# Strassen's token sums before the norm's root, in place; the first two products of two pairs ahead of it; weight sums split anew in each superblock

## The chip, the cores and the metric

The kernel runs on one core of a Trainium2 chip. The core has five engines with instruction queues of their own: TensorE (PE, matrix products, with weight loads listed as PEld), VectorE (DVE), ScalarE (ACT), GpSimd (POOL) and SyncE (SP), which here issues all transfers between DRAM and the on-chip memory (SBUF). Products land in PSUM banks. The metric is the device time of one execution in microseconds (us); the kernel before took 2969.23 us, the median of 3 runs (2965.46 to 2977.01).

## What is computed

One layer of a hybrid encoder, on 2048 prompt tokens and 32 tokens of a running stream, 1024 features wide. Cut to what matters here:

```python
m, k, v, h_fin, ssm_conv_new = mixer(rmsnorm(x, p['g_mix_pre']), ...)
x = x + rmsnorm(m, p['g_mix_post'])
f, ffn_conv_new = conv_ffn(rmsnorm(x, p['g_ffn_pre']), ffn_conv_prev, p)
x = x + rmsnorm(f, p['g_ffn_post'])

def conv_ffn(h, conv_prev, p):
    gu = h @ p['w_up']
    gate, up = gu[..., :D_FF], gu[..., D_FF:]
    gate_c, conv_new = causal_dwconv(gate, conv_prev, p['ffn_conv_w'], p['ffn_conv_b'])
    act = jax.nn.gelu(gate_c, approximate=True) * up
    return act @ p['w_down'], conv_new
```

`rmsnorm(x, g)` is x times g times one over the root of the mean of x squared plus 1e-6, per token. `mixer` ends with an output projection (1024 by 1024). D_FF is 2816, in 22 units of 128. Everything is 32-bit floating point.

## The kernel before

**Precision.** PE multiplies in a rounded 32-bit format. Each operand is therefore split into a high part (a cast) and a low part (the operand less the high part); `dense` (L144 to L159) makes three products of each: high by high, high by low, low by high. A split costs an ACT cast and a subtraction on POOL or DVE (`divide`, L129, for weights; `part`, L1021, for activations).

**Stages.** `phase_in` (attention starts at about 640 us) makes queries, keys, values and the state-space half. Then tokens go in four superblocks (SBS): three of 512 tokens and one of 544. For superblock s, `Tail.stream` does the output projection in two halves of tokens (`out_units`), its norm and the residual addition (`residual`), the feed-forward norm, the up projection with its gate for 22 units j, and the down projection in groups of units (`down`). What is left of the down projection (`owed`) is done in the next superblock's stream, its first eight steps at the start and the rest after the norm. `finish` adds the second residual. The stream of superblock s is a generator: `Attention.heads` takes steps of it between the attention slots of superblock s + 1. Superblock 3 has no attention beside it (`alone`).

**Strassen.** In superblocks 1, 2 and 3 (FAST) gate and up product of a unit are made together in `pair`: the two halves of the tokens and the two halves of the features make a 2 by 2 block product with gate and up weights, done with seven products in place of eight. Products 1 and 2 use the first half's tokens alone; 5 and 3 the difference of the halves; 6, 7 and 4 sums and differences of all four quadrants (m11, m12, m21, m22). `normal` builds these: it takes the norm's root, multiplies the tiles by gain and root, splits the first half (a), and for the second half (b) subtracts, splits and files the operands in `self.X`. Products 3, 5, 6, 7 need sums of weights. Superblock 0, which uses plain products (`up`), makes them from the raw weights (`sums`) and writes them to DRAM (sS). Superblock 1 loads each, splits it and writes the split sum to DRAM (wS_sum); 2 and 3 load these (`factor`).

**Norms.** Squares are made on ACT and added tile by tile on POOL (`square`, L805) into one tile (msq, sq). `rstd_steps` (L181) multiplies it on PE with a column of ones (L192), scales on DVE (L201), takes the power -0.5 on POOL (L211) and spreads the result over the partitions with another product (L223). In superblock 0 the root is not multiplied into the tokens but into the gate after the product (L1222), and its square into the last norm (`finish`, through `cols`).

**Order.** A planner orders each engine's instructions by a simulated timeline, within the dependencies. `pin` and `mark` hold products of PE in written order: each pinned product stays behind the last marked one, so that the dense products keep their order up to superblock 2; attention's own products are marked but not pinned, and can run ahead. In superblock 3 dense products aren't pinned. Tiles with one name share a fixed number of buffers: a new one waits until all readers of the old are done. The raw weights have a ring of 5 (RBUFS), the split ones of 6 (WBUFS), xhi0 to xhi7 and xlo0 to xlo7 one each.

## Time and profile before

| | |
|---|---|
| median of 3 runs | 2969.23 us |
| profiled execution | 2973.12 us (span 2971.3 us) |
| mean granted TensorE clock | 0.967 |
| busy: PE, weight loads | 93%, 82% |
| busy: DVE, ACT, POOL | 63%, 46%, 51% |
| moved to and from DRAM | 725.20 MB, 244 GB/s |

Shares are of the span. PE's busy time is modelled from pipelined products, so that a busy PE need not be at its peak. A line of a timeline has the start and duration in us, the engine, the line of the kernel, the operation with the tile written and the tiles read, its size and its count, and in brackets the idle time ahead of it and what ended that. A line of groups has the count, busy us and mean ns of one, and the idle time ahead. A line of waits has the waiting engine and line, what was waited for, then us in all, times, and the longest. A line of transfers has count, KB each and the median us from issue to landing.

### The profile page before, as it was taken

The numbers are of one execution on the slowest core, as the hardware profiler recorded it, in microseconds if no ns is written. First come the engines' busy times: TensorE is split into PE (matmuls) and PEld (weight loads), VectorE is DVE, ScalarE is ACT, GpSimd is POOL, SyncE is SP. The second block draws the span as 40 slices with busy tenths as digits, with TensorE's granted clock in tenths as the row PEclk, the third lists the DMA queues.
The fourth block names the chain that finished last, engine by engine and source line by source line (L and its number), as shares of the span: only waits on it lengthen the run. The fifth ranks groups of instructions, "written<-read, shape, count | busy, mean of one in ns | idle before, by whom it ended". The sixth has DMA issues, their size and how long they took to land. (4 is left out here: it accounts for less than half of the span.)

```text
span 2971.3 us, 50761 instructions
## 1 busy us (share of the span) xinstructions
PE 2761.0 (93%) x18019; PEld 2451.1 (82%) x18019; DVE 1863.9 (63%) x2915; ACT 1380.9 (46%) x2920; POOL 1521.7 (51%) x1361
## 2 busy tenths in 40 slices
PE   7999999989889999988799999898999999699997
PEld 6777787877778888877689988887999999699997
DVE  7667576547686777637876764478665762634444
ACT  4344444337665555436665553465543553332222
POOL 3555565435776767648665654474422334521213
PEclk9999999989989999999899999999999999799998
DMA  5646464649778888778478898876878777698885
GB/s 177 182 153 174 146 178 126 159 134 291 242 256 285 282 283 286 277 269 270 169 263 314 312 330 294 314 234 195 294 263 276 256 245 263 219 328 267 300 277 180
DMA packets 383806, 725.20 MB, mean 244 GB/s; under 512 B 78938, under 2 KB 198370, under 8 KB 383554
## 3 DMA queue, kind: packets, MB, share of 16 engines
q1 hardware_dynamic: 383554, 721.95, 72.8%
q8 instruction: 144, 2.36, 0.3%
q14 instruction: 108, 0.88, 0.1%
HBM read 526.44 MB, written 195.36 MB: 243 GB/s over the span
## 5 line engine op out<-in xcount | busy, mean ns | idle before, releaser
L150 PE MATMUL o<-xhi,w 128*128 128x256 f32 (+2 forms) x3760 | 916.0, 328 | 37.5 <-ACT xhi L315 8.0
L150 PEld LDWEIGHTS o<-xhi,w 128*128 128x128 f32 x3760 | 648.6, 192 | 103.6 <-issue 9.1
L135 POOL TENSOR_TENSOR w<-wraw,w 128x512 fp32r<-128x512 f32 (+3 forms) x332 | 521.1, 1575 | 288.6 <-ACT w L134 258.0
L150 PE MATMUL o<-xlo,w 128*128 128x256 f32 (+2 forms) x1880 | 613.6, 326 | 6.4 <-DVE xlo L301 4.2
L700 POOL TENSOR_TENSOR beta<-beta,prow 128x512 f32<-128x512 f32 (+3 forms) x256 | 269.4, 1054 | 337.8 <-DVE prow L695 291.9
L150 PEld LDWEIGHTS o<-xlo,w 128*128 128x128 f32 x1880 | 361.2, 192 | 36.3 <-DVE xlo L301 6.1
L150 PE MATMUL o<-ah,w 128*128 128x512 f32 x992 | 343.5, 403 | 10.1 <-DMA w<-wS_dn 5.1
L134 ACT CAST w<-wraw 128x512 fp32r<-128x512 f32 (+3 forms) x332 | 226.0, 683 | 185.3 <-PE o L150 106.8
L695 DVE TENSOR_TENSOR_SCAN prow<-gam,prow,z 128x513 f32<-128x513 f32 x192 | 244.1, 1273 | 32.1 <-ACT beta L693 31.3
L868 DVE TENSOR_TENSOR wt<-pt,wt 128x512 fp32r<-128x512 f32 (+2 forms) x320 | 189.5, 598 | 105.1 <-ACT wt L867 103.7
L150 PEld LDWEIGHTS o<-ah,w 128*128 128x128 f32 x992 | 187.5, 189 | 53.6 <-DVE f L1292 5.8
L150 PE MATMUL u<-xhi,w 128*128 128x256 f32 (+1 forms) x832 | 211.9, 332 | 7.4 <-DVE y L1256 3.3
L692 ACT ACTIVATE gam<-z 128x512 f32<-128x512 f32 (+2 forms) x320 | 173.0, 541 | 77.8 <-PE z L844 45.2
L867 ACT CAST wt<-pt 128x512 fp32r<-128x512 f32 (+2 forms) x320 | 166.6, 527 | 76.9 <-PE pt L863 73.9
L885 PE MATMUL pa<-wt,v 128*64 128x256 f32 (+3 forms) x1152 | 180.6, 287 | 19.9 <-DVE wt L868 9.8
L150 PE MATMUL o<-al,w 128*128 128x512 f32 x496 | 197.4, 398 | 0.0
L863 PE MATMUL pt<-ident,beta 128*128 128x128 f32 x1088 | 182.1, 282 | 10.8 <-DVE beta L700 4.5
L885 PEld LDWEIGHTS pa<-wt,v 128*64 128x64 f32 (+1 forms) x1152 | 150.3, 168 | 38.7 <-DVE wt L868 14.0
L1184 POOL TENSOR_TENSOR y<-y,gb 128x512 f32<-128x512 f32 (+1 forms) x66 | 88.3, 1337 | 169.7 <-ACT gb L1183 169.0
L693 ACT ACTIVATE beta<-z 128x512 f32<-128x512 f32 (+2 forms) x320 | 173.3, 542 | 0.0
L844 PE MATMUL z<-k,qa 128*128 128x512 f32 (+2 forms) x320 | 141.3, 442 | 33.5 <-DVE prow L695 29.6
L150 PE MATMUL t<-ah,w 128*128 128x272 f32 (+1 forms) x768 | 165.1, 303 | 7.2 <-ACT ah L1190 4.2
(326 smaller groups left out, 5952.9 us busy)
## 6 DMA issues: line engine op xcount, KB each, us to landing
w<-wS_up SPq DMA_DIRECT2D x198, 512.0 KB, 5.4
w<-wS_sum SPq DMA_DIRECT2D x176, 512.0 KB, 5.1
w<-wS_dn SPq DMA_DIRECT2D x144, 384.0 KB, 4.2
wS_sum<-w SPq DMA_DIRECT2D x88, 512.0 KB, 6.2
w<-wS_out SPq DMA_DIRECT2D x78, 512.0 KB, 5.8
wS_up<-w SPq DMA_DIRECT2D x66, 512.0 KB, 4.1
wraw<-wup SPq DMA_DIRECT2D x88, 256.0 KB, 4.2
sS<-wraw SPq DMA_DIRECT2D x88, 256.0 KB, 3.2
```

The source lines that it names most:

```text
L134: nc.scalar.copy(hi, raw[:, :m, :])
L135: nc.gpsimd.tensor_tensor(lo, raw[:, :m, :], hi.bitcast(F32), op=ALU.subtract)
L150: mm = nc.tensor.matmul(ps[:, : c1 - c0], l, r, start=first and i == 0 and k == 0, stop=last and i == 2 and k == len(w) - 1, **({"skip_gro ...
L692: nc.scalar.activation(g[:, c0:512], z, AF.Sigmoid, scale=-0.125)
L693: nc.scalar.activation(b[:, :n], z, AF.Sigmoid, scale=0.125)
L695: nc.vector.tensor_tensor_scan(back(pr), back(g), z[:, 0:1].to_broadcast([P, n + 1]), self.kn.ones[:, 0:1] if prev is None else prev, op0= ...
L700: eng.tensor_tensor(b[:, :n], b[:, :n], pr[:, c0 + 1 : 513], op=ALU.mult)
L844: mm = nc.tensor.matmul(z[:, :n], q[:, P * b : P * b + P], k[:, :n], start=e == 0, stop=e == 1 and kc < s)
L863: mm = nc.tensor.transpose(t[:, P * j : P * j + P], w[:, P * j : P * j + P], kn.ident[:])
L867: nc.scalar.copy(hi, t)
L868: nc.vector.tensor_tensor(lo, t, hi.bitcast(F32), op=ALU.subtract)
L885: nc.tensor.matmul(av[:m, 2 * P * p + c0 : 2 * P * p + 2 * P], v[:, j, :m], wt[:, rest, j, c0:], start=kc == s and p + j + rest == 0, stop ...
```

## The change

- **Quadrants in tiles of their own.** `Q` holds four tiles n0 to n3 (half by half of features) where `M` was one; differences are made in place in them, and the operands for products 6, 7 and 4 go to tiles n0 to n6.
- **No root ahead of the sums.** In FAST superblocks `residual` leaves the residual h in the x tile, and ACT writes h times the gain back to the quadrant. `near` splits the first half, `far` subtracts and splits for the second; both split into the tiles of the output projection's input (`cat`) where `normal` and `split` took new ones. `root` sums the squares, which ACT makes in place in the eight h tiles, with eight products per block; POOL's additions go. The output projection's norm sum gets its last square as a second term.
- **Root after the product.** In `pair` the gate is multiplied with the root: its first half on DVE in place of ACT's copy, its second half by one more operation on POOL. The last norm takes the root's column as superblock 0 does.
- **Order.** In FAST superblocks the rest of `owed` comes right after `far`; then the root's sum (pinned), products 1 and 2 of pairs 0 and 1 (AHEAD), and the root's spreading (pinned). `bank` keeps their PSUM banks apart. In superblock 0 the first half's split and root go into the second half of the projection.
- **Weights.** The split sums are written no more; superblocks 1, 2 and 3 each load the raw sums and split them. RBUFS is 4. The tiles msq and sq share one name, and attention takes its own later.

```diff
 WBUFS = 6
-RBUFS = 5
+RBUFS = 4
 FAST = (1, 2, 3)
+AHEAD = 2
...
             for i, t in enumerate(sq):
-                nc.tensor.matmul(
+                mm = nc.tensor.matmul(
                     ps[:q, b : b + 1], t[:, b * P : b * P + q], self.ones[:, 0:1],
                     start=i == 0, stop=i == len(sq) - 1,
                 )
+                if pin and b + i == 0:
+                    self.pin(mm)
+        if pin:
+            self.mark(mm)
...
                 nc.vector.tensor_tensor(att[-1][r, :512], av[0:64, :], att[-1][r, :512], op=ALU.add)
+                if h == 1:
+                    sq = self.tmp.tile([P, 544], F32, name="sq")
...
         if c0 == 0:
-            self.M = self.mp.tile([P, KC, 544], F32, name="m")
-            self.m = [self.M[:, c, :] for c in range(KC)]
-            self.msq = att.tmp.tile([P, 544], F32, name="msq")
+            self.Q = [[self.mp.tile([P, 4, 272], F32, name=f"n{2 * i + e}") for e in range(2)] for i in range(2)]
+            self.msq = att.tmp.tile([P, 544], F32, name="sq")
...
+            nc.scalar.copy(m, ps[:, : c1 - c0])
+            if i < KC - 1:
+                att.square(self.msq[:, c0:c1], m, i == 0)
+            else:
+                t = att.tmp.tile([P, 272], F32, name="sqt", bufs=2)[:, : c1 - c0]
+                nc.scalar.activation(t, m, AF.Square)
+                self.msqs = [self.msq[:, c0:c1], t]
             yield
...
+    def m(self, c, half):
+        c0, c1 = half
+        return self.Q[int(c0 > 0)][c // 4][:, c % 4, : c1 - c0]
 
...
-            eng.tensor_tensor(m[:, c0:c1], m[:, c0:c1], x, op=ALU.add)
-            nc.sync.dma_start(kn.hS[s][:, c, c0:c1], m[:, c0:c1])
-            att.square(self.msq[:, c0:c1], m[:, c0:c1], c == 0, x)
+            h = x if fast else m
+            eng.tensor_tensor(h, m, x, op=ALU.add)
+            nc.sync.dma_start(kn.hS[s][:, c, c0:c1], h)
+            if fast:
+                nc.scalar.activation(m, h, AF.Copy, scale=kn.col(C_GFFN + c))
+            else:
+                nc.scalar.activation(x, m, AF.Square)
+            self.h.append(x)
             yield
...
         kn, nc, att = self.kn, self.kn.nc, self.att
         c0, c1 = half
         if c0 == 0:
-            self.x = kn.parts()
+            self.x = self.cat
...
+            yield
+
+    def root(self, s, half, pin=False):
...
-        kn.rstd_narrow(att.tmp, *kn.bank, [self.msq[:, c0:c1]], c1 - c0, D, out=self.r[:, c0:c1], rcol=col)
         self.cols[s, c0] = col
+        yield from kn.rstd_steps(
+            att.tmp, *kn.bank, self.h, c1 - c0, D, out=self.r[:, c0:c1], rcol=col, pin=pin
+        )
 
...
-    def normal(self, s, half):
-
...
+    def squares(self):
+        for h in self.h:
+            self.kn.nc.scalar.activation(h, h, AF.Square)
+
+    def near(self, s, half):
+
+        kn, nc = self.kn, self.kn.nc
+        c0, c1 = half
+        hi, lo = self.x = self.cat
+        for k in range(KC):
+            self.part(self.m(k, half), hi[k][:, c0:c1], lo[k][:, c0:c1], nc.vector if k % 2 else None)
+            yield
+
+    def far(self, s, half):
+
+        kn, nc = self.kn, self.kn.nc
         c0, c1 = half
         n = c1 - c0
...
+        (b11, b21), (b12, b22) = self.Q
+        two = slice(0, 2), slice(2, 4)
+        sub = lambda out, a, b, k: nc.vector.tensor_tensor(out[:, k, :n], a[:, k, :n], b[:, k, :n], op=ALU.subtract)
+        for k in two:
+            sub(b12, b12, b11, k)
+        for k in range(KC):
+            self.part(self.m(k, half), hi[k][:, c0:c1], lo[k][:, c0:c1], nc.vector if k >= 4 else None)
         self.X = {}
-        for i, src in zip(put, raw):
-            h, l = put[i][:, :, :n], put[i][:, :, n : 2 * n]
-            for e in range(2):
-                k = slice(2 * e, 2 * e + 2)
-                self.part(src[e], h[:, k, :], l[:, k, :], nc.vector)
-            self.X[i] = [h[:, k, :] for k in range(4)], [l[:, k, :] for k in range(4)]
+
+        def put(i, src, h, l, eng):
+            h, l = (self.mp.tile([P, 4, 272], F32R, name=f"n{e}") for e in (h, l))
+            self.part(src[:, :, :n], h[:, :, :n], l[:, :, :n], eng)
+            self.X[i] = [h[:, k, :n] for k in range(4)], [l[:, k, :n] for k in range(4)]
+
+        for k in two:
+            sub(b22, b22, b12, k)
+        put(6, b22, 2, 4, nc.vector)
+        for k in two:
+            sub(b11, b22, b11, k)
+        for k in two:
+            sub(b21, b22, b21, k)
+        put(7, b11, 3, 5, nc.gpsimd)
+        put(4, b21, 0, 6, nc.vector)
         side = lambda ks, c: ([hi[k][:, c : c + n] for k in ks], [lo[k][:, c : c + n] for k in ks])
         self.X |= {1: side(range(4), 0), 2: side(range(4, 8), 0), 3: side(range(4, 8), n), 5: side(range(4), n)}
 
...
-        key = ("sum", j, i)
-        if key in kn.kept:
-            return kn.recall(self.ring(), [key], 4, self.slot())
-        return kn.divide(self.ring(), kn.raw(self.raws[j, i][:], 4), 4, key if s < NSB - 2 else None, self.slot())
+        return kn.divide(self.ring(), kn.raw(self.raws[j, i][:], 4), 4, None, self.slot())
...
-        k = self.n_bank % (5 if self.keep else 3)
+        k = max(self.n_bank, 0) % (5 if self.keep else 3)
...
-        for i in (1, 2, 5, 6, 3, 7, 4) if j == 0 else (1, 5, 6, 2, 3, 7, 4):
+        for i in (1, 2, 5, 6, 3, 7, 4) if j < AHEAD else (1, 5, 6, 2, 3, 7, 4):
...
             elif i == 2:
-                nc.scalar.copy(gb[:, 2 : 2 + h], b)
+                nc.vector.tensor_tensor(gb[:, 2 : 2 + h], b, self.r[:, :h], op=ALU.mult)
             elif i == 3:
                 e = min(nt, 512) - h
-                add(gb[:, 2 + h : 2 + h + e], b[:, :e], t[:, :e])
+                add(t, b, t)
+                mul = lambda out, c: nc.gpsimd.tensor_tensor(out, t[:, c], self.r[:, h:nt][:, c], op=ALU.mult)
+                mul(gb[:, 2 + h : 2 + h + e], slice(0, e))
                 if last:
-                    add(gb[:, 516:548], b[:, e:], t[:, e:])
+                    mul(gb[:, 516:548], slice(e, h))
...
+    def ready(self, s, half):
+        if s in FAST:
+            self.squares()
+            yield from self.near(s, half)
+        else:
+            yield from self.split(s, half)
+        yield from self.root(s, half)
...
-        chain = chained(self.residual(s, a), self.normal(s, a) if fast else ())
+        chain = chained(self.residual(s, a), self.ready(s, a))
         for n, _ in enumerate(self.out_units(s, cat, b)):
             yield
-            if n % 4 == 0 or fast and n % 4 == 2:
+            if n % 2 == 0:
                 next(chain, None)
         for _ in chain:
...
-        if not fast:
-            self.root(s, a)
-        for _ in self.residual(s, b):
-            pass
+        self.finished(self.residual(s, b))
+        early = []
         if fast:
-            for _ in self.normal(s, b):
-                pass
+            self.squares()
+            self.far(s, b)
+            yield from owed
+            root = self.root(s, b, pin=True)
+            next(root)
+            acts = {0: []}
+            self.n_bank = -4
+            early = [self.pair(s, j, acts[0]) for j in range(AHEAD)]
+            for p in early:
+                yield from islice(p, 4)
+            next(root)
         else:
-            self.split(s, a)
-            self.split(s, b)
-            self.root(s, b)
-        yield from owed
+            self.finished(self.split(s, b))
+            self.finished(self.root(s, b))
+            yield from owed
+            acts = {0: []}
         done = iter(())
```

75 lines of the change are left out of this document (26 added, 49 removed).

## Prediction

> **What bounds the kernel now.** I read the page first: the span, and PE's busy share in forty slices.
>
> ```profile
> span 2971.3 us, 50761 instructions
> ...
> PE   7999999989889999988799999898999999699997
> ```
>
> TensorE (PE) is the bound: busy in nine tenths or more of nearly every slice. A change gains where PE is empty or at half clock, and costs where it gives PE work or stops feeding it. Slices 12, 20, 28 and 35 (74 us each) hold the places where a superblock passes from the output projection to the feed-forward network (I call them **transitions**). I then read the busy time of each engine in those stretches. The columns are stretch, length, busy us (instructions) of PE, weight loads, DVE, ACT, POOL, then granted clock, DMA share, GB/s.
>
> ```profile
> 840.00:870.00 30.00, 18.79 (x78) 14.23 (x77) 28.16 (x48) 18.34 (x47) 18.94 (x22) 0.67 0.64 217
> 1380.00:1450.00 70.00, 50.71 (x274) 38.24 (x273) 63.73 (x89) 49.54 (x114) 47.36 (x54) 0.86 0.45 152
> 1970.00:2030.00 60.00, 46.32 (x261) 36.75 (x260) 56.68 (x84) 42.29 (x99) 42.96 (x49) 0.93 0.48 152
> 2530.00:2600.00 70.00, 47.18 (x260) 43.05 (x258) 43.75 (x87) 21.09 (x54) 40.53 (x49) 0.73 0.65 207
> ```
>
> I count as lost the length less PE busy times the clock: 30 - 18.79*0.67 = 17.4 for superblock 0, 70 - 50.71*0.86 = 26.4 for 1, 60 - 46.32*0.93 = 16.9 for 2, 70 - 47.18*0.73 = 35.6 for 3: **96 us** in all. The timelines of superblock 3 (start, duration, engine, line) show what the loss is made of.
>
> ```profile
> 2521.48 0.29 PE L150 MATMUL t<-xhi,w 128*128 128x272 f32 x1
> ...
> 2545.42 0.29 PE L150 MATMUL t<-xhi,w 128*128 128x272 f32 x1
> 2556.69 1.15 PE L192 MATMUL u<-ones,msq 128*128 128x1 f32 x6 [10.98 <-POOL msq L805]
> ```
> ```profile
> 2527.18 3.28 ACT L1024 CAST xhi<-m 128x272 fp32r<-128x272 f32 x8 [4.46 <-DVE m L1038]
> ```
> ```profile
> 2547.54 0.43 DVE L992 TENSOR_TENSOR m<-m,xr 128x272 f32<-128x272 f32 x1
> ...
> 2560.71 3.36 DVE L1038 SCALAR_TENSOR_TENSOR m<-m,cv,u 128x272 f32<-128x272 f32 x8 [2.61 <-issue]
> 2563.98 1.30 DVE L1051 TENSOR_TENSOR m<-m 128x1088 f32<-128x1088 f32 x1
> ...
> 2582.03 0.71 DVE L1025 TENSOR_TENSOR t<-ub,t 128x544 fp32r<-128x544 f32 x1
> ```
> ```profile
> 2553.39 3.25 POOL L805 TENSOR_TENSOR msq<-msq,xr 128x272 f32<-128x272 f32 x4
> ...
> 2563.37 3.44 POOL L1025 TENSOR_TENSOR xlo<-m,xhi 128x272 fp32r<-128x272 f32 x3 [4.27 <-ACT xhi L1024]
> ```
>
> The output projection ends at 2521.8. Only then does ACT cast the *first* half's tiles (2527.18): `normal` takes a new generation of the xhi and xlo tiles, of which there is one each, and the projection still reads the old one. The residual's last addition ends at 2547.97. PE, busy until then with the down projection still owed, stands from 2545.7 and gets the sum of squares only at 2556.69, when POOL has added the last squares (L805). Root and broadcast last until 2560.7, then eight multiplications on DVE, a subtraction, splits and two more levels of differences, the last split (t) ending at 2582.7. Superblock 1 has the same chain between attention slots:
>
> ```profile
> 1388.29 0.41 DVE L992 TENSOR_TENSOR m<-m,gb 128x256 f32<-128x256 f32 x1
> ```
> ```profile
> 1423.65 0.50 PE L192 MATMUL u<-ones,msq 128*128 128x1 f32 x4
> ...
> 1451.23 0.28 PE L150 MATMUL o<-xhi,w 128*128 128x256 f32 x1
> ```
>
> The residual's last addition ends at 1388.7, the sum starts 35 us later, and the first product behind it runs at 1451.23. Outside the transitions PE is nearly full:
>
> ```profile
> 890.00:1290.00 400.00, 396.66 (x1901) 323.08 (x1900) 275.83 (x342) 203.41 (x426) 270.39 (x220) 1.00 0.82 283
> 1460.00:1900.00 440.00, 411.05 (x2840) 373.29 (x2839) 279.26 (x391) 226.92 (x486) 258.36 (x220) 0.99 0.87 310
> 2060.00:2440.00 380.00, 376.57 (x2664) 346.88 (x2663) 248.21 (x363) 178.93 (x386) 129.27 (x123) 1.00 0.80 269
> 2650.00:2900.00 250.00, 249.22 (x1982) 248.81 (x1981) 109.86 (x233) 61.59 (x134) 52.80 (x45) 1.00 0.83 285
> ```
>
> Idle there is 400 - 396.66 = 3.3 us in superblock 0's feed-forward part, 29.0 in 1's, 3.4 in 2's, 0.8 in 3's. Superblock 1 differs from 2 in that it splits the weight sums and writes them; that is the state into which the change puts 2 and 3, without the writes.
>
> **The change part by part.** The sum is made against the profiled execution, 2973.1 us (span 2971.3), which is 3.9 above the median of the runs shown, 2969.2.
>
> *Transitions.* Two things change. First, the splits are written into the projection's own input tiles, so the first half's casts, low parts and root no longer wait for the projection's end; they go under its second half, where PE is full and the other engines aren't. Second, the subtractions no longer wait for the root: the residual times the gain goes straight to them (L1038's multiplications go, ACT scales instead), the squares go to ACT, and PE sums eight square tiles where POOL did seven additions. In superblock 3 the second takes 2556.6 - 2548.0 = 8.7 us of POOL, 4.1 of root and broadcast and 3.4 of multiplications off the products' path, 16 us; the first takes the 3.3 us of casts, with their low parts, from in front of the residual, which can add some 5 us earlier, near 2543. Left are one subtraction (1.3) and the first splits (3.44 us for three low parts on POOL here), so product 5 can run near 2548; then three more subtractions at 1.3 and whole-tile casts and low parts of about 3 us each in turn, the last near 2560 instead of 2582. PE fills from 2545.7 with two products of two pairs: 48 matmuls, by the last stretch above (250 us for 1982) 0.126 us each, 6 us. Of 35.6 lost I take away 26, leaving some idle and about 10 us of half clock. In superblock 1 attention shares DVE (63.7 of 70 busy); the difference chain, some 10 us of DVE (four subtractions at 1.3, and low parts), takes about 20 there, so products near 1405 instead of 1451: 20 of 26.4, and in proportion, rounded down, 12 of 16.9 in superblock 2. Superblock 0 gains by the first half's splits alone: 9 of 17.4. **-67**, bounds -30 and -86 (all but 10).
>
> A wait is added here: the squares overwrite h, so ACT must wait for h's way to DRAM.
>
> ```profile
> w<-wS_sum SPq DMA_DIRECT2D x176, 512.0 KB, 5.1
> wS_sum<-w SPq DMA_DIRECT2D x88, 512.0 KB, 6.2
> ...
> hS<-m SPq DMA_DIRECT2D x48, 128.0 KB, 4.2
> ```
>
> That is 4.2 us to landing, and behind a waiting square stand ACT's casts for the differences and attention's sigmoids; for these squares waits the sum, and in superblocks 1 and 2, where PE's order is fixed, both pairs' early products behind the sum. The down projection still owed by the superblock before covers it; without that cover it costs 4 us each, inside the bounds.
>
> The TensorE clock shows in the rows: 0.73 over superblock 3's transition. The Trainium skill, page "TensorE: Matmul & The Clock Gate", section "What's actually happening", says that an idle window of about 3.4 us halves the clock; if no gap that long were left, superblock 3 would keep full clock, and by that rule the sum would be 5 us lower (half of the 10 us that I left at half clock). The trace agrees so far that a gap of 11 us stands ahead of the low clock.
>
> *More work on PE.* Each root sums eight tiles instead of one, and the output norm's sum gets a second term.
>
> ```profile
> 2520.69 0.63 PE L192 MATMUL u<-ones,msq 128*128 128x1 f32 x6
> 2521.26 0.39 PE L150 MATMUL t<-xlo,w 128*128 128x272 f32 x1
> ```
>
> Six instructions take 2521.26 - 2520.69 = 0.57, 0.095 each; two per block and tile. Added: 28 for each half of 256 tokens (six), 42 for each of 272 (two), and 4 or 6 more for the second term: 252 + 36 = 288, 27 us. The first halves' 13.7 fall between dense products and count whole; of the second halves' I count 5, since PE is empty there otherwise. **+19**, bounds 14 and 27.
>
> *Weight sums.* Gone: 88 writes and 176 loads of 512 KB, the loads now 176 of 256 KB raw. In superblock 1 PE waited for loads, and SP's queue stood behind those writes:
>
> ```profile
> PE o L150 <- DMA w<-wS_up: 6.6, 7, 2.1
> ...
> PE o L150 <- DMA w<-wS_dn: 5.1, 1, 5.1
> ```
> ```profile
> SPq L138 <- POOL w L135: 81.8, 47, 6.6
> ```
>
> 11.7 us of PE's 29.0; superblock 2, with neither splits nor writes, idles 3.4 in all. I take **-9** (0 to -12). Added in superblocks 2 and 3: 88 splits each, at the cost shown in 1:
>
> ```profile
> L135 POOL TENSOR_TENSOR w<-wraw,w 128x512 fp32r<-128x512 f32 x83 | 115.8, 1406 | 51.1 <-ACT w L134 46.5 <-DMA w<-wS_up 4.2 <-DMA wraw<-sS 0.4
> ...
> L1166 POOL TENSOR_TENSOR ub<-ub 128x256 f32<-128x256 f32 x22 | 17.5, 795 | 13.6 <-DVE ub L1133 11.3 <-DVE rn_v L201 1.3 <-DMA wS_sum<-w 1.1
> ```
> ```profile
> L134 ACT CAST w<-wraw 128x512 fp32r<-128x512 f32 x81 | 49.8, 621 | 63.4 <-PE o L150 52.4 <-DMA wS_sum<-w 5.5 <-PE u L150 4.3
> ```
>
> That is 88 * (1.406 POOL + 0.621 ACT) = 124 and 55 us in each. POOL rises in superblock 2's stretch from 129 to 129 + 76*1.406 + 19*0.795 = 251 of 380 (66%; 1 has 59%), in 3's from 53 to 149 of 250. Both fit, but POOL works in order: a split stands behind y's product (waiting for ACT's sigmoid), and attention's beta product behind splits. Of superblock 1's 29.0 idle, 17 is not loads; I carry half, **+8** (0 to 25) for 2 and, with no attention there, **+3** (0 to 45) for 3.
>
> DVE pays too. The gate's taps in superblock 1, then in 2:
>
> ```profile
> L1177 DVE SCALAR_TENSOR_TENSOR y<-gb,cv,y 128x512 f32<-128x512 f32 x44 | 49.9, 1134 | 15.1 <-ACT y L1175 14.7
> ...
> L1185 DVE TENSOR_TENSOR y<-ub,y 128x512 f32<-128x512 f32 x22 | 24.6, 1119 | 24.0 <-POOL y L1184 24.0
> ```
> ```profile
> L1177 DVE SCALAR_TENSOR_TENSOR y<-gb,cv,y 128x512 f32<-128x512 f32 x38 | 31.9, 840 | 7.0 <-ACT y L1175 6.6
> ...
> L1185 DVE TENSOR_TENSOR y<-ub,y 128x512 f32<-128x512 f32 x19 | 14.7, 774 | 7.1 <-POOL y L1184 7.1
> ```
>
> (1.134 - 0.840)*44 + (1.119 - 0.774)*22 = 20.5 us of DVE per superblock, on 248 of 380: covered by DVE's idle time.
>
> *Raw ring of four.* Superblock 0 holds four raw tiles per step until the sums are out; the fifth served for loading ahead.
>
> ```profile
> SPq L114 <- DMA sS<-wraw: 35.8, 40, 2.8
> ```
>
> SP already waits for a release 40 times, yet PE idles 3.3 us in 400. **+3**, bounds 0 and 25 (1.1 us in each of 22 steps).
>
> *Gate in the pair.* One copy moves from ACT to DVE; a POOL multiplication of 0.8 us (L1166's kind) enters the gate's chain, hidden while the pair's results are used a group later. At the very end it isn't:
>
> ```profile
> PE t L150 <- ACT ah L1190: 4.2, 1, 4.2
> ```
>
> **+1** on that wait (0 to 2). The dearer last scale with the root's column, and the shared sq tile, cost nothing: they lie beside dense work.
>
> Sum: -67 + 19 - 9 + 8 + 3 + 3 + 1 = **-42**; 2973.1 - 42 = 2931, and 2927 against the median.
>
> **The rivals.** (1) *The transitions close.* Only 10 us of the 96 stay: -86 in place of -67, -61 in all, 2908. For it: 20 us of chain gone and 6 us of early work in each. Against: DVE at 91% in superblock 1's. (2) *The gain arrives by half.* The squares wait for h's landing, the sum holds the fixed order, the early products come no earlier than their successors would: -30, and SP's waits only change their names (0 for -9): -30 + 19 + 8 + 3 + 3 + 1 = +4, 2973. (3) *POOL late with the splits, slower.* Superblock 2 takes 1's idle rate, 29.0*380/440 = 25, and in superblock 3 each of 22 pairs waits for two splits in a row, 2*(1.406 + 0.621) = 4.1 us: 89. Then -67 + 19 - 9 + 25 + 89 + 3 + 1 = +61, 3030. With 25 in superblock 2 it decides from (67 - 19 + 9 - 25 - 3 - 1)/22 = 1.3 us of wait per pair on. For it: POOL's queue is in order; against: the split's own waits (46.5 us on ACT) hurt PE little in 1. (4) *DVE shut out.* If each split stopped a DVE operation of two SBUF inputs for its whole length, superblock 2 would get 88*1.406 = 124 on DVE's 248 of 380: DVE full, and PE would lose as in a transition; taking a tenth of 380, +38 for +8, 2957. The rows speak against it: 20.5 us, not 124. This is the rule of the Trainium skill, "SBUF — State Buffer", section "Who interferes with whom": a DVE instruction with two SBUF inputs and a POOL instruction that reads SBUF block each other entirely; the trace shows the lengthening, but an overlap only now and then.
>
> **How the numbers follow.** Forecast 0.42 (its own range 2915 to 2950), rival 1 0.20, rival 2 0.17, rival 3 0.15, rival 4 0.06. About 0.5%, 15 us, is what a measurement of this kernel tells from no change, so faster means under 2954, slower over 2984. Faster: 0.39 of the forecast, rival 1 whole, 0.02 of 4: 0.61. Slower: 0.14 of rival 3 and 0.03 of rival 2: 0.17. The rest 0.22. The range from 2900 to 2990 leaves out some 0.07 at rival 1's end and 0.13 at rival 3's; the bounds of the transitions, the ring and superblock 2's splits, one at a time, lie inside it, superblock 3's 45 too.
>
> **What would show it.** Right: in superblock 3 the first half's casts run under the output projection, the last difference split ends within 20 us of the residual's last addition (35 now), the transitions lose 30 us or so, superblock 1's load waits shrink, PE idle in 2's and 3's stretches stays below 12. Wrong: PE waiting for L135 in superblocks 2 or 3, DVE above 80% there, PE gaps in superblock 0's steps behind SP's releases, or the root's sum standing in front of idle PE.

## The result, and the profile after

The changed kernel takes **2983.38 us** (median of 8 runs, 2980.06 to 2989.66) beside 2972.86 for the kernel before on the same chip (8 runs, 2965.46 to 2977.01): ratio **1.0038** [1.0026, 1.0051]. It is slower by 0.4%, less than the 0.5% that the prediction counted as no change. I forecast 2927, 1.4% faster; the measured time lies in the range (2900 to 2990), which reaches to both sides of the kernel before, but on the other side of it. Below, every run stands by its ratio to the kernel before on the same chip; 0.1% is 3 us.

First the changed kernel's page (span, and PE's busy share in forty slices).

```profile
span 2980.7 us, 51672 instructions
...
PE   7999999989899999999899999998999999789997
```

Slices 12, 20, 28 and 35, the transitions, show 9, 8, 8 and 7 (8, 7, 8 and 6 before); slice 36, just behind the last of them, fell from 9 to 8. The transitions by the columns of the prediction (stretch, length, busy us of PE, weight loads, DVE, ACT, POOL, clock, DMA share, GB/s):

```profile
840.00:870.00 30.00, 26.08 (x155) 22.68 (x154) 24.76 (x45) 19.94 (x50) 14.46 (x16) 0.83 0.77 259
1375.00:1445.00 70.00, 65.86 (x436) 58.27 (x435) 58.13 (x80) 49.90 (x123) 53.64 (x57) 0.95 0.66 214
1945.00:2005.00 60.00, 56.45 (x360) 50.86 (x359) 54.79 (x77) 42.65 (x101) 43.67 (x42) 0.91 0.52 170
2510.00:2580.00 70.00, 60.29 (x415) 55.23 (x413) 45.52 (x68) 31.14 (x73) 56.57 (x55) 0.97 0.66 207
```

Length less PE busy times the clock gives 30 - 26.08*0.83 = 8.4, 70 - 65.86*0.95 = 7.4, 60 - 56.45*0.91 = 8.6 and 70 - 60.29*0.97 = 11.5: **36 us lost in place of 96**. (Of superblock 3's 11.5, some 5 are the start of the gap of 6.36 us that is followed below and that runs past the end of this stretch.) The transitions shorten as the change meant them to. The same view of the feed-forward stretches shows who took it back.

```profile
880.00:1280.00 400.00, 384.16 (x1821) 310.95 (x1819) 255.80 (x325) 194.41 (x405) 249.84 (x209) 0.99 0.78 269
1450.00:1860.00 410.00, 397.33 (x2773) 363.65 (x2772) 290.96 (x406) 215.12 (x460) 260.79 (x232) 0.98 0.67 216
2020.00:2440.00 420.00, 409.98 (x2882) 376.42 (x2881) 310.66 (x426) 234.05 (x494) 265.20 (x235) 0.99 0.64 206
2560.00:2620.00 60.00, 42.94 (x294) 41.53 (x294) 44.35 (x60) 22.15 (x48) 48.45 (x44) 0.86 0.68 224
2620.00:2930.00 310.00, 297.55 (x2313) 294.79 (x2312) 152.73 (x256) 105.06 (x213) 176.19 (x152) 0.98 0.62 198
```

PE idles 15.8 us in superblock 0 (3.3 before), 12.7 in 1 (29.0), 10.0 in 2 (3.4) and 17.1 + 12.5 = 29.5 in 3 (before, 2.0 in the 60 us from 2595, where its pairs begin, and 0.8 in the 245 behind them, at a clock of 1.00). In superblock 3 the clock fell with the gaps, to 0.86 in the first 60 us. There POOL is busy 48.45 of 60 and 176.19 of 310 us; before it was 52.80 of 250. The worst gap of superblock 3, in the timelines of PE, then ACT, then DVE, shows how it arises:

```profile
2581.24 0.59 PE L151 MATMUL t<-xhi,w 128*128 128x272 f32 x1 [6.36 <-ACT ub L1176]
```
```profile
2580.26 0.65 ACT L1216 CAST ah<-y 128x544 fp32r<-128x544 f32 x1 [6.68 <-DVE y L1213]
2580.81 0.38 ACT L1176 COPY ub<-t 128x272 f32<-128x272 f32 x1
```
```profile
2570.00 7.92 DVE L1345 SCALAR_TENSOR_TENSOR f<-f,cv,rstd 128x256 f32<-128x256 f32 x8
2577.85 1.21 DVE L1211 TENSOR_TENSOR y<-ub,y 128x512 f32<-128x512 f32 x1
2578.98 1.25 DVE L1213 TENSOR_TENSOR y<-ub,y 128x32 f32<-128x32 f32 x1
```

PE stood 6.36 us for an ACT copy that frees a PSUM bank (`ub`, L1176). That copy stood in ACT's queue behind the cast of a gate (`ah`, L1216), that cast waited for DVE's gate product (L1211, L1213), and the product stood in DVE's queue behind eight multiplications of the finish (L1345), 7.92 us together. All three operations are longer here than elsewhere. In the kernel before, the eight multiplications take 4.71 us, and in the changed kernel's next pair, with POOL idle beside it, the second product (L1213) takes 0.19:

```profile
2585.24 4.71 DVE L1319 SCALAR_TENSOR_TENSOR f<-f,cv,rstd 128x256 f32<-128x256 f32 x8 [0.24 <-ACT rstd L229]
```
```profile
2591.81 0.19 DVE L1213 TENSOR_TENSOR y<-ub,y 128x32 f32<-128x32 f32 x1
```

In the gap that product, of 32 columns, took 1.25 us and ended at 2580.2, just when the split that POOL ran beside it ended (start 2578.47, 1.71 us). It was held, not slowed. So the question for the experiments was which part of the change makes DVE late, and what the other costs are.

### The profile page after: what moved, and what is told of

Its sections match the earlier page's. It is cut to its first block, busy times and chain, and to the rows that moved or that the text cites. A ratio compares the mean times of both kernels' runs of the same rounds, so it can differ in the third digit from the quotient of the medians.

```text
span 2980.7 us, 51672 instructions
## 1 busy us (share of the span) xinstructions
PE 2791.3 (94%) x18307; PEld 2485.9 (83%) x18307; DVE 1947.4 (65%) x2920; ACT 1464.4 (49%) x3075; POOL 1770.3 (59%) x1552
## 5 line engine op out<-in xcount | busy, mean ns | idle before, releaser
L136 POOL TENSOR_TENSOR w<-wraw,w 128x512 fp32r<-128x512 f32 (+3 forms) x508 | 768.1, 1520 | 401.3 <-ACT w L135 372.4
L135 ACT CAST w<-wraw 128x512 fp32r<-128x512 f32 (+3 forms) x508 | 335.0, 663 | 314.9 <-PE o L151 136.6
L709 POOL TENSOR_TENSOR beta<-beta,prow 128x512 f32<-128x512 f32 (+3 forms) x256 | 261.8, 1024 | 233.0 <-DVE prow L704 202.3
L877 DVE TENSOR_TENSOR wt<-pt,wt 128x512 fp32r<-128x512 f32 (+2 forms) x320 | 190.3, 598 | 83.6 <-ACT wt L876 82.9
L151 PE MATMUL o<-n,w 128*128 128x256 f32 (+1 forms) x1404 | 190.3, 285 | 4.3 <-DVE y L1157 2.5
L1203 DVE SCALAR_TENSOR_TENSOR y<-gb,cv,y 128x512 f32<-128x512 f32 (+1 forms) x132 | 169.7, 1285 | 27.3 <-ACT y L1201 20.4
L151 PEld LDWEIGHTS o<-n,w 128*128 128x128 f32 x1404 | 179.0, 190 | 6.0 <-DVE y L1157 2.8
```

The costliest lines, as they stand in the source:

```text
L135: nc.scalar.copy(hi, raw[:, :m, :])
L136: nc.gpsimd.tensor_tensor(lo, raw[:, :m, :], hi.bitcast(F32), op=ALU.subtract)
L151: mm = nc.tensor.matmul(ps[:, : c1 - c0], l, r, start=first and i == 0 and k == 0, stop=last and i == 2 and k == len(w) - 1, **({"skip_gro ...
L709: eng.tensor_tensor(b[:, :n], b[:, :n], pr[:, c0 + 1 : 513], op=ALU.mult)
L877: nc.vector.tensor_tensor(lo, t, hi.bitcast(F32), op=ALU.subtract)
L1203: nc.vector.scalar_tensor_tensor(y[:, :W], gb[:, i : i + W], kn.col(wc + i), y[:, :W], op0=ALU.mult, op1=ALU.add)
```

## The experiments

### What the split weight sums cost, and how

Four kernels: the changed one with the sums kept again; the kernel before without keeping them; and two that keep one part of each split and make the other, so that ACT's cast and POOL's subtraction are apart.

```diff
-        return kn.divide(self.ring(), kn.raw(self.raws[j, i][:], 4), 4, None, self.slot())
+        key = ("sum", j, i)                      # e1: as before the change
+        if key in kn.kept:
+            return kn.recall(self.ring(), [key], 4, self.slot())
+        return kn.divide(self.ring(), kn.raw(self.raws[j, i][:], 4), 4, key if s < NSB - 2 else None, self.slot())
```

> The changed kernel with one part undone: the split weight sums are kept again (superblock 1 splits them and writes both parts to DRAM, superblocks 2 and 3 load them back). Theory A (the transitions gave what they were to give, and the gain was spent on the splits in superblocks 2 and 3): superblock 3's stretch of pairs loses some 20 us of TensorE time again in place of 60, superblock 2's some 18 in place of 33, superblock 1's some 43 in place of 31, so the time falls by 40 to 50 us to about 2938 us (2928 to 2950). Rival B (the gate's new multiplications by the root, on POOL and DVE, slow the pairs whatever the weights do): superblock 3 still loses 50 us or more and the time stays at 2970 to 2985 us.

2951.72 us, ratio 0.995 [0.9934, 0.9966]: 0.88% below the changed kernel, **26 us**. Theory A holds in kind; the fall is less than its 40 to 50 us.

```diff
 # e3: in the kernel before
-        ... 4, key if s < NSB - 2 else None, self.slot())
+        ... 4, None, self.slot())
```

> The kernel before with one part of the change alone: no split weight sum is kept, superblocks 1 to 3 each load the raw sum and split it. Theory A (the splits by themselves cost superblock 3 some 40 us and superblock 2 some 15, and superblock 1 gains some 10 from the writes that fall away): about 3015 us (3000 to 3030). Rival B (only together with the multiplications by the root do the splits overload POOL, DVE and ACT): 2965 to 2985 us.

2980.41 us, 1.0035 [1.0017, 1.0053]: 10 us. That is inside rival B's range and far below theory A's, but the reason that B gives, that the splits cost only together with the multiplications by the root, is not what the stages show. The table has the us from the first tap of one superblock to the first tap of the next, by the profiled execution of each kernel (a **tap** is one of the two operations per pair on DVE that make the gate's convolution, L1177 in the kernel before, L1203 in the changed one):

| from first tap | before | e3 | difference | e1 | changed kernel | difference |
|---|---|---|---|---|---|---|
| superblock 1 to 2 | 582.8 | 562.7 | -20 | 574.7 | 566.8 | -8 |
| superblock 2 to 3 | 550.8 | 555.7 | +5 | 538.5 | 552.8 | +14 |
| superblock 3 to the end | 375.3 | 399.7 | +24 | 392.4 | 419.5 | +27 |

In superblock 3 the splits cost 24 us by themselves and 27 in the changed kernel, the same within some 5 us. The net is smaller in the kernel before since superblock 1 gains more there when its writes fall away. The same pair of kernels with seven raw buffers (e11 and e8, below) gives -5, +14 and +32. DVE's groups in superblock 3 (busy us, mean ns of one, idle before), in the kernel before, in e3, in the changed kernel and in e1:

```profile
L1177 DVE SCALAR_TENSOR_TENSOR y<-gb,cv,y 128x546 f32<-128x546 f32 x38 | 35.1, 923 | 3.8 <-ACT y L1175 3.3
L1292 DVE TENSOR_TENSOR f<-t,f 128x272 f32<-128x272 f32 x80 | 34.9, 440 | 57.0 <-PE t L150 56.9
```
```profile
L1177 DVE SCALAR_TENSOR_TENSOR y<-gb,cv,y 128x546 f32<-128x546 f32 x36 | 49.4, 1371 | 9.0 <-ACT y L1175 8.6
```
```profile
L1203 DVE SCALAR_TENSOR_TENSOR y<-gb,cv,y 128x546 f32<-128x546 f32 x34 | 47.1, 1386 | 7.5 <-ACT y L1201 7.2
L1318 DVE TENSOR_TENSOR f<-t,f 128x272 f32<-128x272 f32 x80 | 33.9, 438 | 39.5 <-PE t L151 39.4
```
```profile
L1206 DVE SCALAR_TENSOR_TENSOR y<-gb,cv,y 128x546 f32<-128x546 f32 x36 | 33.6, 933 | 2.3 <-ACT y L1204 2.0
```

The gate's taps, two operands from SBUF, take 923 ns with kept sums and 1371 with splits in the kernel before, 933 and 1386 in the changed one; the down projection's sum, one operand from PSUM, takes 440 and 438. So the splits lengthen the taps by half, and the gate's multiplications by the root don't.

```diff
 # e5 (e6): the sum's high (low) part is written in superblock 1 and loaded in 2 and 3; there:
+        raw = kn.raw(self.raws[j, i][:], 4)
+        w = kn.held(self.ring(), self.slot())
...
+            nc.sync.dma_start(hi.bitcast(F32), kn.kept[key][:])                          # e6: lo
...
+            nc.gpsimd.tensor_tensor(lo, raw[:, :, :], hi.bitcast(F32), op=ALU.subtract)  # e6: nc.scalar.copy(hi, raw[:, :, :])
```

> The changed kernel, but of each split weight sum the high part is kept: superblock 1 writes it to DRAM, superblocks 2 and 3 load it beside the raw sum, so ACT has no cast there and POOL still subtracts to make the low part. The bytes loaded are those of the kernel that keeps both parts (2951.7 us). Theory A (what the splits cost is POOL's subtraction, during which DVE's operations with two operands in SBUF run slower): the gate's taps on DVE in superblock 3 stay near 1380 ns and the time stays at 2972 to 2985 us. Rival B (what they cost is ACT's cast, which stands in ACT's queue ahead of the copies that free PSUM): the time falls to 2950 to 2960 us.

> The counterpart: the low part of each sum is kept and loaded beside the raw sum, ACT casts the high part as in the changed kernel, POOL has no subtraction for it in superblocks 2 and 3. Theory A (POOL's subtraction): the taps come back to some 930 ns and the time falls to 2950 to 2960 us. Rival B (ACT's cast): the taps come back too, but TensorE still waits for ACT's copies and casts and the time stays at 2970 to 2985 us.

e5, POOL's subtraction without the cast: 3008.33 us, 1.0131 [1.0102, 1.0161], 28 us *above* the changed kernel. e6, the cast without the subtraction: 2950.66 us, 0.9943 [0.9923, 0.9964], the same as with both parts kept; its taps:

```profile
L1216 DVE SCALAR_TENSOR_TENSOR y<-gb,cv,y 128x546 f32<-128x546 f32 x36 | 34.3, 953 | 2.4 <-ACT y L1214 2.0
```

ACT's 176 casts add nothing to the net, and POOL's subtractions make all of it: theory A. One thing is not held equal: in superblock 1, e1 writes both parts and e6 one, so a cost of the casts of up to some 8 us (the table's gain without the writes) could hide in that; in superblock 3, where nothing is written, e6 takes 392.5 us by the table's measure and e1 392.4. That e5 came out above the changed kernel neither theory had; its taps take 1190 ns, and in its trace POOL's subtractions wait long for the loaded part:

```profile
L1131 POOL TENSOR_TENSOR w<-wraw,w 128x512 fp32r<-128x512 f32 x68 | 98.0, 1456 | 73.1 <-DMA w<-wK 62.5 <-issue 3.1 <-PE t L151 3.0
```

They wait 62.5 us in this stretch, with the gate's work on POOL queued behind; that this makes the difference to the changed kernel is likely, but not shown. Next the same subtractions on DVE:

```diff
 # e9: eng is nc.vector in superblocks 2 and 3
-        nc.gpsimd.tensor_tensor(lo, raw[:, :m, :], hi.bitcast(F32), op=ALU.subtract)
+        (eng or nc.gpsimd).tensor_tensor(lo, raw[:, :m, :], hi.bitcast(F32), op=ALU.subtract)
```

> The changed kernel with the low parts of the split weight sums in superblocks 2 and 3 made by DVE in place of POOL; loads, casts and products are the same. It tells whether the splits cost by what POOL does to DVE or by the order of POOL's own queue and DVE's load. Theory A (while POOL subtracts, DVE's operations with two SBUF operands are held up; a subtraction on DVE itself, some 690 ns by the gate's product of 512 columns, costs less than that): the taps in superblock 3 come back to some 930 ns and the time falls to 2955 to 2970 us. Rival B (DVE has no room for 150 more subtractions of 0.7 us each, waiting for ACT's casts in its queue): 2985 us or more.

2955.37 us, 0.9953 [0.9936, 0.9971], theory A: the time is that of the kept sums again, though every split is still made (and, as in e6, without all of e1's writes, so that a few us can hide here too). The taps take 1005 ns and a subtraction 828:

```profile
L136 DVE TENSOR_TENSOR w<-wraw,w 128x512 fp32r<-128x512 f32 x65 | 53.4, 828 | 26.9 <-ACT w L135 26.6
...
L1203 DVE SCALAR_TENSOR_TENSOR y<-gb,cv,y 128x546 f32<-128x546 f32 x36 | 36.2, 1005 | 1.0 <-ACT y L1201 0.6
```

That leaves these ways for POOL's subtraction to cost: beside DVE's operations, through POOL's own queue, or through products that wait for a late low part. Two kernels keep the sums and add a subtraction whose result nobody reads.

```diff
 # e10: from a constant          e13: from the two loaded parts, in place of c, c
...
+            o = kn.wp.tile([P, kn.unit, P], F32, name="wraw", bufs=kn.rbufs)
+            kn.nc.gpsimd.tensor_tensor(o[:], c, c, op=ALU.subtract)
```

> The changed kernel with the split sums kept (2951.7 us) and, beside each recall of one in superblocks 2 and 3, a subtraction on POOL of the split's size whose result nobody reads (from a constant, into a raw weight buffer that is idle there). So POOL's work is that of the splits, but no product waits for it and it waits for no load. Theory A (POOL's subtraction costs by running beside DVE and by filling POOL): the taps lengthen to 1300 ns or more and the time rises by 20 us or more, to 2972 us or more. Rival B (the splits cost because a product waits for a late low part, or POOL stands waiting for a raw sum with the gate's work behind it): 2950 to 2960 us, whatever the taps do.

3045.07 us, 1.0255 [1.0239, 1.0272]. That lies in theory A's range, but the time can't be set against the splits': all 176 subtractions, tied to no load, ran between 1864.3 and 2300 us, superblock 3's too, so that theory A's taps of 1300 ns there can't be judged either. But the trace has DVE's same operations in superblock 2 with them (2060 to 2290) and without (2320 to 2500):

```profile
L1209 DVE SCALAR_TENSOR_TENSOR y<-gb,cv,y 128x512 f32<-128x512 f32 x14 | 15.0, 1069 | 0.4 <-ACT y L1207 0.2
...
L877 DVE TENSOR_TENSOR wt<-pt,wt 128x512 fp32r<-128x512 f32 (+3 forms) x53 | 33.6, 635 | 25.7 <-ACT wt L876 25.5
```
```profile
L1209 DVE SCALAR_TENSOR_TENSOR y<-gb,cv,y 128x512 f32<-128x512 f32 x19 | 14.2, 749 | 2.2 <-ACT y L1207 1.9
...
L877 DVE TENSOR_TENSOR wt<-pt,wt 128x512 fp32r<-128x512 f32 (+3 forms) x19 | 12.1, 635 | 2.5 <-ACT wt L876 2.5
```

The taps take 1069 and 749 ns, though these subtractions take nothing from DVE's work and give nothing to it; L877, which takes an operand from PSUM, takes 635 both times. The subtractions aren't the only work on POOL in the first stretch. Tap by tap, the 19 of the second stretch and 2 of the first have nothing on POOL beside them and take 0.74 to 0.75 us; the other 12 have POOL's work beside them, these subtractions or the layer's own, and take 0.77 to 1.55. That is the rule of the Trainium skill, page "SBUF — State Buffer", section "Who interferes with whom" (a DVE instruction with two SBUF inputs contends with a POOL instruction that reads SBUF; one with at most one doesn't, outside the modes that use two ports), and this trace agrees: 1.43 times as long in the mean.

> The changed kernel with the split sums kept (2951.7 us) and a subtraction of the split's size on POOL for each recalled sum of superblocks 2 and 3, from the two loaded parts into a raw weight buffer that is idle there. It runs when the load has landed, so it is spread over the pairs as the splits are; no product waits for its result and no cast stands before it. Theory A (the splits cost by POOL's subtraction running beside DVE and filling POOL): the taps in superblock 3 lengthen to 1250 ns or more and the time comes to 2972 us or more. Rival B (they cost by POOL's queue standing at a late cast and by products waiting for a late low part): 2950 to 2962 us, with the taps lengthened or not.

3009.57 us, 1.0136 [1.0119, 1.0153]: 55 us above e1, more than the splits' 26, with no cast and no product behind it. Theory A by the time; the taps, 1227 ns, stay just short of its 1250. Taps and POOL in superblock 3:

```profile
L1210 DVE SCALAR_TENSOR_TENSOR y<-gb,cv,y 128x546 f32<-128x546 f32 x32 | 39.3, 1227 | 5.7 <-ACT y L1208 5.0
```
```profile
L1127 POOL TENSOR_TENSOR wraw<-w 128x512 f32<-128x512 f32 x67 | 97.2, 1466 | 68.2 <-DMA w<-wS_sum 68.2
```

So late low parts aren't needed to explain the cost. Two causes are left: DVE's longer operations, and POOL's queue standing at a load (68.2 us here; in the changed kernel 67.0 at casts) with the gate's work behind. The traces tell how much each adds to a pair's gate in superblock 3, from its first tap to the end of its low part on POOL (means of 22 pairs): 11.0 us in e1, 12.9 in the changed kernel. DVE's part of that grew by 1.9 us (taps, from the first's start to the second's end, 2.1 to 3.4; L1208 0.75 to 0.95; the last products 1.0 to 1.4), the two waits of the gate's work for POOL by 0.5 (0.3 and 0.3 us to 0.7 and 0.4), and other steps shrank by 0.5. In e13 these waits are 1.3 and 0.6. So in the changed kernel DVE's longer operations are the larger part of the chain's growth; how the 26 us of the kernel's time divide is not shown.

### What the ring of four costs

```diff
 # e2: in the kernel before
-RBUFS = 5
+RBUFS = 4
 # e8: in the changed kernel, kn.raw(); spare is set in superblock 0 alone
+        self.n_raw += 1
+        if self.spare is not None and self.n_raw % 7 > 3:
+            raw = self.spare.tile([P, 4, 272], F32, name=f"n{self.n_raw % 7}")[:, :, :P]
```

> The kernel before with one part of the change alone: four buffers in place of five in the ring of raw weight tiles. Theory A (the smaller ring is what costs superblock 0 its 20 us, the weight loads land late and ACT's cast waits for them with the gate's work queued behind it): superblock 0's feed-forward loses some 30 us of TensorE time in place of 9, and the time rises to about 2990 us (2982 to 3000). Rival B (the ring is free, superblock 0 is longer because of the order in which its transition leaves the queues): 2973 us, within 5.

> The changed kernel with seven raw weight buffers in superblock 0 (four of the ring and three tiles that hold the differences in later superblocks and are idle in this one); nothing else. Theory A (four buffers cost superblock 0 between 11 us, as in the kernel before with four, and 17 us, what its stretch grew by): 2965 to 2973 us. Rival B (in the changed kernel superblock 0 is slow for the order of its queues as well): 2978 us or more, TensorE still losing 30 us or more in that stretch.

e2: 2980.43 us, 1.0045 [1.0028, 1.0062], **13 us** for that one number, between theory A's range and rival B's. e8: 2962.12 us, 0.9975 [0.9961, 0.9989], **19 us** below the changed kernel, a little more than theory A's. ACT's casts in superblock 0 (880 to 1280 us), in the kernel before, e2, the changed kernel and e8 (its ring, then its three spare tiles):

```profile
L134 ACT CAST w<-wraw 128x512 fp32r<-128x512 f32 x80 | 49.6, 620 | 68.2 <-PE o L150 32.9 <-DMA wraw<-wup 14.1 <-POOL w L135 6.4
```
```profile
L134 ACT CAST w<-wraw 128x512 fp32r<-128x512 f32 x78 | 48.5, 624 | 72.9 <-DMA wraw<-wup 52.4 <-PE o L150 15.1 <-DMA sS<-wraw 2.0
```
```profile
L135 ACT CAST w<-wraw 128x512 fp32r<-128x512 f32 x78 | 48.8, 626 | 78.7 <-DMA wraw<-wup 51.0 <-PE o L151 14.1 <-DMA qb<-qS 5.0
```
```profile
L140 ACT CAST w<-wraw 128x512 fp32r<-128x512 f32 x44 | 27.1, 618 | 33.8 <-PE o L156 31.3 <-POOL w L141 1.5 <-DMA sS<-n 0.9
L140 ACT CAST w<-n 128x512 fp32r<-128x512 f32 x33 | 20.4, 618 | 30.2 <-PE o L156 14.0 <-DMA n<-wup 6.5 <-POOL w L141 4.4
```

With four buffers the casts wait some 51 us for the raw weights (52.4 and 51.0) where they waited 14.1 with five; with seven 6.5 are left. In ACT's queue the attention's and the gate's work stands behind such a cast. In the stretch PE is busy 396.66, 387.55, 384.16 and 396.05 us of 400. That is theory A's cause; in the kernel before the cost is smaller than it said.

### What the root's eight-tile sums cost

```diff
 # e4
-            att.tmp, *kn.bank, self.h, c1 - c0, D, out=self.r[:, c0:c1], rcol=col, pin=pin
+            att.tmp, *kn.bank, self.h[:1], c1 - c0, D, out=self.r[:, c0:c1], rcol=col, pin=pin
```

> The changed kernel with part of the computation left out: the root's sum takes one of the eight tiles of squares, so the norm ahead of the feed-forward is wrong in size; 7 of every 8 of these small matmuls are gone, some 250 in eight sums, nothing else. Theory A (the added sums are TensorE work on the path, a weight load of 190 ns and a matmul behind it each): the time falls by 20 to 30 us, to about 2958 us. Rival B (they fill time in which TensorE would wait for the gate's first products or the next cast): it falls by under 10 us, to 2975 us or more.

2947.58 us, 0.9931 [0.991, 0.9952]: 1.07% below the changed kernel, **32 us**, a little over theory A's 20 to 30. By the pages PE's busy time fell as much, from 2791.3 to 2759.6 us, and in the changed kernel's trace PE nowhere waits for one of these squares, so what e4 saves is the work and not a wait. The second halves' sums are no longer in an empty place, as PE's timeline in superblock 3 shows:

```profile
2538.95 0.28 PE L193 MATMUL u<-ones,xr 128*128 128x1 f32 x2
2539.09 0.37 PE L151 MATMUL t<-xlo,w 128*128 128x272 f32 x1
...
2539.55 2.55 PE L193 MATMUL u<-ones,xr 128*128 128x1 f32 x34
```

Products run before and between them. Can POOL add the squares instead?

```diff
 # e7: on e1; squares() of both halves (superblock 0's squares are added too); second half's sum behind four early products
...
+            self.kn.nc.scalar.activation(q if h is self.h[0] else h, h, AF.Square)
+            if h is not self.h[0]:
+                self.kn.nc.gpsimd.tensor_tensor(q, q, h, op=ALU.add)
```

> The changed kernel with the split sums kept (2951.7 us) and the root's sum over one tile again: POOL adds the eight squares, in the second half behind the casts of the differences, and the sum of the second half is taken behind the first two products of the two early pairs. Theory A (the eight-tile sums are TensorE work on the path, 30 to 36 us in all, and POOL has room for the adds): 2918 to 2928 us. Rival B (the adds hold back POOL's low parts, of the first half's under the output projection above all, so that the transitions take back half or more): 2937 us or more.

2943.75 us, 0.9925 [0.9905, 0.9945]: only 7 us below e1, in the bounds of rival B. PE's busy time on the page fell from 2779.3 (e1) to 2761.1 us, 18 us, so more than half of it came back as idle time. POOL isn't a free place for these adds.

### Do the costs add, and do two early pairs matter

> The changed kernel with both of these undone at once: the split sums kept, and seven raw buffers in superblock 0. If the costs found so far add (32 us for the splits, 21 for the ring) the time is about 2931 us (2925 to 2938), and what is left, 38 to 42 us faster than before, is the shorter transitions less the eight-tile root sums. If both meet the same slack it stays at 2945 us or more.

> As the run before (kept sums, seven raw buffers), and the squares of each superblock's first half are added by POOL into one tile, under the output projection; the second half keeps its eight small sums, since its adds were on the path in the kernel that had them in both halves. Theory A (the first half's sums are pure TensorE work under other products, some 12 to 15 us in four superblocks, and POOL's adds are covered there): 2915 to 2922 us. Rival B (the adds delay the first half's low parts on POOL, and the casts behind them): 2930 us or more.

> The kernel with kept sums and seven raw buffers (2924.8 us), but only one pair's first two products, in place of two pairs', stand ahead of the rest at each of the three transitions. Twelve split products of 287 to 292 ns per factor, two factors, make some 7 us of TensorE work per transition that is moved from behind the last low parts to ahead of them. Theory A (they fill TensorE while DVE and POOL make the last low parts): 10 to 20 us slower, 2935 to 2945 us. Rival B (one pair's products suffice, the casts of the differences are done when they end): within 6 us of 2924.8.

e11 (the edits of e1 and e8): 2924.77 us, 0.9864 [0.9836, 0.9892]; 1.73% below the changed kernel, 52 us, where splits and ring by themselves gave 26 + 19; they add, and do not meet the same slack. e12 (besides, e7's adds in the first halves alone): **2915.83 us, 0.9819** [0.98, 0.9838], the fastest, 1.8% below the kernel before; by the medians 9 us below e11, less than the 12 to 15 expected, and the two intervals touch. e14 (e11 with `AHEAD = 1`, one early pair): 2921.27 us, 0.9832 [0.9813, 0.9852], the same as e11 within the intervals: the second early pair gives nothing that can be measured, rival B.

## Why the prediction was wrong

**Right: the transitions.** -67 was forecast, and by the prediction's own view 96 - 36 = 60 us went (65, if the gap's start is left out). What it named is in the timelines of superblock 3, ACT's first and then DVE's:

```profile
2493.70 0.42 ACT L1055 CAST xhi<-n 128x272 fp32r<-128x272 f32 x1
...
2514.62 0.39 ACT L978 COPY n<-t 128x272 f32<-128x272 f32 x1 [3.29 <-PE t L151]
...
2531.04 0.43 ACT L1060 ACTIVATE xr<-xr 128x272 f32<-128x272 f32 x1 [1.13 <-DMA hS<-xr]
```
```profile
2531.64 0.43 DVE L1015 TENSOR_TENSOR xr<-n,xr 128x272 f32<-128x272 f32 x1
...
2554.95 1.29 DVE L1056 TENSOR_TENSOR n<-n,n 128x1088 fp32r<-128x1088 f32 x1 [2.84 <-ACT n L1055]
```

The first half's casts (L1055) stand ahead of the projection's last copy (L978), and the squares' wait for h's way to DRAM (L1060) is 1.13 us, on ACT (2.8 at the most in the other superblocks). The last difference split ends 24 us after the residual's last addition, not within 20; products run meanwhile, and PE's longest gap there is 2.74 us. Of the early products, the second pair's gave nothing (e14). On the clock, the transition, the stretch ahead of the gap of 6.36 us and the one behind it:

```profile
2510.00:2560.00 50.00, 46.97 (x313) 42.35 (x311) 30.53 (x50) 24.12 (x59) 36.57 (x36) 0.97 0.71 222
2560.00:2575.00 15.00, 13.32 (x105) 12.88 (x104) 9.99 (x14) 7.03 (x14) 15.00 (x16) 1.00 0.62 197
...
2583.00:2600.00 17.00, 13.60 (x88) 13.27 (x88) 10.95 (x19) 6.11 (x13) 11.37 (x11) 0.73 0.76 253
```

The granted clock goes from 1.00 to 0.73 over the gap, while over the transition, up to 2560, it was 0.97, with no idle time above 2.74 us there (0.73 before, with a gap of 10.98). The rule of the Trainium skill that the prediction weighed, "TensorE: Matmul & The Clock Gate", section "What's actually happening" (an idle window of about 3.4 us halves the clock), agrees with both.

**Wrong: the splits of superblock 3.** The term was +3 (0 to 45), and the sum for weight sums -9 + 8 + 3 = +2; measured is +26 by the medians. By the table of the first taps (profiled executions, +33 together) the writes gave -8 where I had -9, the splits of superblock 2 cost 14 where I had 8, and those of superblock 3 cost **27 where I had 3**. The step that failed is the one on DVE: I found that the taps lengthen where POOL splits (1.134 in place of 0.840 us), added that up to 20.5 us per superblock, and called it covered by DVE's idle time. That is a reckoning of throughput. DVE was indeed never full, 152.73 of 310 us. But the gate is a chain over POOL, ACT and DVE, in whose queues the copies that free PSUM stand too, and a pair has 16 us here (38 taps, two a pair, in 310 us before), 20 in superblock 2 (38 in 380). The chain grew by 0.46 us per tap, and by more where the finish of the superblock before falls in (L1345), and PE met it: a pair's gate takes 1.9 us longer, most of it on DVE. I had taken superblock 3 as the safe place because it has no attention; by the rows it was the place with the least time per pair, and POOL's share rose there from 21 to 57% (52.80 of 250, 176.19 of 310). The sign that I named, PE waiting for the split itself, nearly didn't show: the waits carry the names of ACT and DVE.

**Rivals.** 36 us stay of the 96, not the 10 of rival 1 nor the 66 of rival 2. Rival 2's sum, +4, is the nearest of the five to the measured +11, but by terms that didn't come: that is luck. Rival 3 put the cost in superblock 3, and in its direction, but by two late splits a pair; e13 shows the cost without late splits. Rival 4 had the mechanism, a split that stops DVE's operations with two SBUF operands, in superblock 2 and by DVE being full; I gave it 0.06 since the lengthening there was small. What the runs show is 4's mechanism, DVE's operations held beside POOL's, at 3's place; that it works by latency is shown for the one gap followed above, fits the longer chain of all 22 pairs, and is argued for the rest of the lost time.

**Wrong in size.** *PE work*, +19 (14 to 27), measured +32: I counted 5 of the second halves' part because PE is empty there otherwise, but the change itself had filled that place, and each of e4's 252 small products cost 0.13 us, where I had read off 0.095. *The ring*, +3 (0 to 25), measured +13 alone and +19 in the changed kernel: I read PE's idle time of 3.3 us as slack in the loads, though the row of SP's 40 waits said that there was none.

The sum with what was measured: transitions -60 to -65, PE work +32, weight sums +26, ring +13 to +19, together +6 to +17; the kernel shows +11. Superblock 1's stretch from 1470 to 1850 us, in the kernel before, in e3 (no writes), in e1 (the change, with the writes) and in the changed kernel:

```profile
1470.00:1850.00 380.00, 358.36 (x2451) 323.51 (x2450) 250.32 (x347) 202.01 (x434) 222.01 (x189) 0.99 0.86 306
```
```profile
1470.00:1850.00 380.00, 370.10 (x2594) 341.36 (x2593) 247.73 (x343) 202.18 (x435) 231.82 (x196) 0.99 0.69 222
```
```profile
1470.00:1850.00 380.00, 370.31 (x2573) 336.26 (x2572) 274.46 (x383) 212.03 (x454) 238.82 (x213) 1.00 0.86 304
```
```profile
1470.00:1850.00 380.00, 371.13 (x2614) 341.22 (x2613) 263.67 (x367) 197.93 (x424) 239.74 (x213) 1.00 0.68 220
```

PE idles 21.6, 9.9, 9.7 and 8.9 us. By idle time alone the change gains with the writes what the kernel before gains without them, and leaving them out besides would bring only 1 us more; but PE gets through 2614 instructions there in place of e1's 2573, and by the table superblock 1 is 8 us shorter. So the idle time doesn't show all that the writes cost. What in the change closes the idle time with the writes kept is open. Each of these numbers is good to some 5 us.

## What to carry to other kernels

Where a change moves work onto an engine that is half idle, price the chain that runs through its queue and through its neighbours' in the stretch with the least time per step, not its share of the span. On this kernel the weight sums' subtraction, moved from POOL to DVE, gave 25 us back, though DVE then does more (186.05 of 310 us in superblock 3 in place of 152.73). When a change closes a gap, recount every cost that was called free because it lay in that gap.

## What the runs showed of the hardware

An operation of DVE with two SBUF operands can be held for as long as POOL's operation runs: 128x32 took 0.19 us with POOL idle and 1.25 beside a split. POOL's own time depends on the company too: the same split took 1.29 us and 1.78 us in one transition of the changed kernel, the longer one beside DVE's subtractions, and DVE's subtraction of 128x544 took 0.71 us by itself and 4.07 us for three there.

```profile
2542.97 1.78 POOL L136 TENSOR_TENSOR w<-wraw,w 128x512 fp32r<-128x512 f32 x1
...
2553.74 1.29 POOL L136 TENSOR_TENSOR w<-wraw,w 128x512 fp32r<-128x512 f32 x1
```
```profile
2534.18 0.71 DVE L1079 TENSOR_TENSOR n<-n,n 128x544 f32<-128x544 f32 x1
...
2542.45 4.07 DVE L1079 TENSOR_TENSOR n<-n,n 128x544 f32<-128x544 f32 x3
```

I had not expected a subtraction that nobody reads to cost more than the split that it stands for (55 us against 26).
